# Where x and u tiles begin in the state buffer, against the weights, in a two-layer trunk kernel

## The chip, the cores and the metric

The kernel runs on one core of a Trainium2 chip. The metric is the device time of one execution in microseconds; the time before is the median of three runs, and the profile is one further execution of the same program.

## The reference, cut to what matters

The input is x of 512 frames by 1024 features, float32. Layer 0 is a gated linear recurrence (HGRN2), layer 1 differential attention over one shared K/V; each is followed by a squared-ReLU MLP of width 4096. Every sub-layer has an RMSNorm before and after it.

```
def squared_relu_mlp(h, w_up, w_down):
    u = jax.nn.relu(h @ w_up)
    return (u * u) @ w_down

for layer in range(2):
    mix = hgrn2_mixer(rms_norm(h, a_norm_pre), ...) if layer == 0 else diff_attn_mixer(rms_norm(h, b_norm_pre), k_sh, v_sh, ...)
    h = h + rms_norm(mix, post)
    h = h + rms_norm(squared_relu_mlp(rms_norm(h, mlp_norm_pre[layer]), w_up, w_down), mlp_norm_post[layer])
    if layer == 0:
        k_sh, v_sh = shared_kv(h, kv_norm, w_kv)
```

## The kernel before, in words

Activations are kept transposed: features on the 128 partitions, frames along the row. Every large product is taken in three float32r matmuls, because each operand is split into a rounded part (hi) and the rest (lo): weights hi by x hi, weights hi by x lo, weights lo by x hi (`mm3`). Each of the three loads its 128 by 128 stationary operand anew (LDWEIGHTS) and streams 512 or 256 columns of the moving one.

The tiles that TensorE reads:
- `xhi0..3` and `xlo0..3`, the sub-layer's input, each 128 by 2 by 512 float32, that is 4096 bytes on each partition.
- `uhi0..3` and `ulo0..3`, of the same size: the mixer's output or the MLP's u. `xraw0..3` (the raw input) and `sums1`, `sums2` lie in the same places at the start, and the attention keeps q and k of some heads there.
- `whi` and `wlo`, the split weights, 4096 bytes each, eight buffers of each, in the pool `wp`.
- `t{layer}_{n}`, the block sums of x for three quarters of each MLP's first product, which is taken with seven instead of eight block products (`sums_x`, `Pair`). They lie in the pool of the MLP under the tag `big`. For the first layer's gates and values the block sums lie in buffers of the weights, and one in `uhi3` and `ulo3`.

Tiles are placed one after the other in the order in which they are made, each rounded up to 32 bytes. The pool `cp` holds `gn`, then x, u and small tables, then comes `wp`. In the kernel before, the sizes in `cp` add up so that every tile of x, u, `t` and the weights begins at the same place modulo 512 bytes. A matmul's operands begin at multiples of 512 bytes within their tiles, so the moving operand and the weights that are loaded during it begin at the same place modulo 512 bytes too.

In nearly all these products the weights are stationary and x, u or `t` moves. In the products for the values (`xmm`: tiles `i`, `is`, `v`) x is stationary and the weights move.

The order of the matmuls on TensorE is fixed when the program is written out, by a planner (`Plan`) with estimated durations; the other engines' instructions are put in order by the framework. `by_halves` and the first MLP quarter run over 256 frames at a time; the MLP's second product (`dn`) runs over 512 columns in three quarters of four.

The recurrence of head h ends with three matmuls into the PSUM tile `st{h}`, an ACT copy and two VectorE operations that make the running state `st{h}` in the state buffer (lines 888 to 896, two buffers), and then seven matmuls `o`, three of which read `st{h}` (lines 898 to 903). Heads come in pairs; where both heads of a pair are ready at once, the second head's `st` is made before the first head's `o`.

`ones1` is a 128 by 128 table of ones beside `onesd`, a table of 1/1024. `ones1` serves three small products: line 769 (the first reciprocal norm, spread over the partitions), line 414 (its columns) and line 788 (lambda). Each is copied out of PSUM by VectorE.

Of the kernel before, what the change touches and what calls it, by code (L numbers as in the profile page):

```python
# [9 lines left out]
F32 = mybir.dt.float32  # L10
F32R = mybir.dt.float32r
# [3 lines left out]
ALU = mybir.AluOpType  # L15
AX = mybir.AxisListType

P = 128
D = 1024
S = 512  # L20
# [24 lines left out]
class Plan:  # L45
# [11 lines left out]
    def until(self, *keys):  # L57
        return lambda: all(k in self.done for k in keys)
# [30 lines left out]
def trunk_kernel(ctx: ExitStack, tc: tile.TileContext, x_t, w_qf, w_g, w_gs, w_i, w_is, w_ao, w_kv, w_q, w_bo, w_up, w_us, w_dn,  # L89
# [3 lines left out]
    cp = ctx.enter_context(tc.tile_pool(name="cp", bufs=1))  # L93
# [4 lines left out]
    def mmt(name):  # L98
        return pm.tile([P, 512], F32, tag="mm", name=name, bufs=4)

    def smt(name):
        return pm.tile([P, 512], F32, tag="sm", name=name, bufs=4)

    v, a, g = nc.vector, nc.scalar, nc.gpsimd
# [16 lines left out]


    gn = cp.tile([P, G_N + 14], F32, name="gn")[:, :G_N]
    xhi = [cp.tile([P, 2, S], F32R, name=f"xhi{i}") for i in range(4)]
    xlo = [cp.tile([P, 2, S], F32R, name=f"xlo{i}") for i in range(4)]
    xraw = [cp.tile([P, 2, S], F32, tag=f"uhi{i}", name=f"xraw{i}", bufs=1) for i in range(4)]
    uhi = [cp.tile([P, 2, S], F32R, tag=f"uhi{i}", name=f"uhi{i}", bufs=1) for i in range(4)]
    sums = [cp.tile([P, 4, 256], F32, tag=f"ulo{i}", name=f"sums{i}", bufs=1) for i in (1, 2)]
    ulo = [cp.tile([P, 2, S], F32R, tag=f"ulo{i}", name=f"ulo{i}", bufs=1) for i in range(4)]

    res = [x_t.rearrange("(k p) t -> p k t", p=P)[:, :, lo:hi] for lo, hi in ((0, 256), (256, 512))]
    a.dma_start(gn, gains)
# [1 line left out]
    mask = cp.tile([P, len(LEVELS), 64], U8, name="mask")  # L134
    onesd = cp.tile([P, P], F32, name="onesd")
    v.memset(onesd, 1.0 / D)
    ones1 = cp.tile([P, P], F32, name="ones1")
    v.memset(ones1, 1.0)
    lb = cp.tile([P, NH], F32, name="lb")
    oml = cp.tile([P, NH], F32, name="oml")  # L140
    rb = cp.tile([P, S], F32, name="rb")
    rcol = cp.tile([P, 4], F32, name="rcol")
# [8 lines left out]
    nlam = cp.tile([P, 1], F32, name="nlam")  # L151
# [111 lines left out]
    def mean_cols(parts, n, ones):  # L263

        ps = smt("ps_mc")[:, :n // P]
        for t in range(n // P):
            for i, sq in enumerate(parts):
                pe.matmul(ps[:, t:t + 1], sq[:, t * P:(t + 1) * P], ones[:, 0:1], start=(i == 0), stop=(i == len(parts) - 1))
        return ps
# [15 lines left out]
    def rsqrt_rows(tmp, ms, add):  # L285

        n = ms.shape[1]
        y, t = tmp
        if add is None:
            a.activation(y, ms, AF.Ln, bias=epsc)  # L290
        elif isinstance(add, float):
            x = ms
            a.activation(y, x, AF.Ln)
        else:
            x = add
            v.tensor_tensor(x, ms, add, op=ALU.add)
            a.activation(y, x, AF.Ln)
        a.activation(y, y, AF.Exp, scale=-0.5)
        if add is None:
            v.scalar_tensor_tensor(t, ms, EPS, y, op0=ALU.add, op1=ALU.mult)  # L300
        else:
            v.tensor_tensor(t, x, y, op=ALU.mult)
        v.tensor_tensor(t, t, y, op=ALU.mult)
        v.scalar_tensor_tensor(y, t, -3.0, y, op0=ALU.add, op1=ALU.mult)
        return y

    def bounds(pool, ps_list, zacc, h, gpost, eab, want, name, gpre=None):

        lo, hi = halves[h]
        n = hi - lo  # L310
# [94 lines left out]
        if want == "ea":  # L405

            a.activation(ea[:, lo:hi], ms, AF.Square, scale=math.sqrt(EPS), bias=eps15)
        else:
            s = rsqrt_rows((tmp[:, 3, 0], tmp[:, 3, 1]), ms, None)
            a.activation(rb[:, lo:hi], s, AF.Copy, scale=-0.5)  # L410
            yield W_RSTD
            pc = smt("ps_rc")
            for i in range(n // P):
                pe.matmul(pc[:, i:i + 1], rb[0:1, lo + i * P:lo + (i + 1) * P], ones1[0:1, 0:1], start=True, stop=True)
            v.tensor_copy(rcol[:, lo // P:hi // P], pc[:, :n // P])
        done(("r", name, h))

    def by_halves(wt, xh, xl, name, before_last=()):
# [36 lines left out]
    def block(pool, proj, gpost, name, layer, want):  # L455

        gpre = gn[:, G_MPRE[layer]:G_MPRE[layer] + 8]
        zacc = pool.tile([P, 8, S], F32, name=f"zacc{layer}")
        last_u = []
        h = 0  # L460
        for r in proj:
            if isinstance(r, list):
                spawn(bounds(pool, r, zacc, h, gpost, None, "ea", name, gpre), 0.3)
                h += 1
            else:
                yield r
# [119 lines left out]
        for q in range(4):  # L586
            if q == 0:
                wt = [load_w(w_up[layer, i], 512, None, f"up{layer}_{i}") for i in range(2)]
                for h, (lo, hi) in enumerate(halves):
                    yield until(("x", name, h))  # L590
                    for pr in range(4):
                        ps = mmt(f"up{layer}_{h}_{pr}").rearrange("p (j t) -> p j t", j=2)
                        for j in range(2):
                            n = 2 * pr + j
# [7 lines left out]
            if q < 3:  # L602
                for i in range(2):
# [6 lines left out]
                    for kt, n4 in order:  # L610
                        wmm(pss[n4], wt, kt, n4 * P, uhi, ulo, 0, S, kt == 0, kt == 7)
                        if kt == 7:
                            n = 4 * i + n4
# [6 lines left out]
            else:  # L620
                wt = load_both(w_dn[layer, q], None, f"dn{layer}_{q}_", last_u[0])
                h = 0
# [70 lines left out]
    def squares(hp, xs):  # L693

        sq = [hp.tile([P, 2, S], F32, tag="vt", name=f"sqx{pr}", bufs=3) for pr in range(4)]
        with tc.issue_after(last_split[0].ins):
            for pr in range(4):
                a.activation(sq[pr], xraw[pr], AF.Square)
        for pr in range(1, 4):
            v.tensor_tensor(sq[0], sq[0], sq[pr], op=ALU.add)  # L700
        return sq[0]
# [43 lines left out]
    def start(hp, xs, maskf):  # L745


        lbe = cp.tile([P, NH], F32, name="lbe")
        lbz = cp.tile([P, NH], F32, name="lbz")
        alb = gn[:, G_LB:G_LB + NH]  # L750
        v.tensor_tensor(lbe, alb, alb, op=ALU.subtract)
        a.activation(lbe, lbe, AF.Exp)
        v.reciprocal(lbz, lbe)
        v.tensor_tensor(lbe, lbe, lbz, op=ALU.mult)
        v.tensor_tensor(lb, lbe, lbe, op=ALU.subtract)
        v.tensor_scalar(oml, lb, -1.0, 1.0, op0=ALU.mult, op1=ALU.add)
        v.tensor_copy(mask, maskf)
        yield until("w1")
        ssum = squares(hp, xs)
        yield W_XSUM  # L760
        rsqrt_col(mean_cols([ssum[:, j, :] for j in range(2)], S, onesd), EPS, rcol, aside=True)
        v.tensor_scalar(nrcol, rcol, -1.0, None, op0=ALU.mult)
        done("rcol")

        dg = hp.tile([P, 4, P], F32, tag="os", name="dg", bufs=2)
        v.tensor_tensor(dg, ident.unsqueeze(1).to_broadcast([P, 4, P]), rcol.unsqueeze(2).to_broadcast([P, 4, P]), op=ALU.mult)
        yield W_XRSTD
        ps = smt("ps_sp")
        pe.matmul(ps, ones1, dg.rearrange("p c t -> p (c t)"), start=True, stop=True)
        v.tensor_copy(rb, ps)  # L770
        done("rb")

    def params(hp):

        lp = hp.tile([1, 256], F32, name="lp")
        a.dma_start(lp, lam_p)
        lpv = lp.rearrange("p (a b d) -> p a b d", a=2, b=2)
        pr_ = lpv[:, :, 0, :]
        v.tensor_tensor(pr_, pr_, lpv[:, :, 1, :], op=ALU.mult)
        l2 = hp.tile([1, 2], F32, name="l2")  # L780
        v.tensor_reduce(l2, pr_, axis=AX.X, op=ALU.add)
        a.activation(l2, l2, AF.Exp)
        l1 = hp.tile([1, 1], F32, name="l1")
        v.tensor_tensor(l1, l2[:, 0:1], l2[:, 1:2], op=ALU.subtract)
        v.tensor_scalar(l1, l1, LAM_INIT, -1.0, op0=ALU.add, op1=ALU.mult)
        yield 15.0
        psl = smt("psl")
        pe.matmul(psl[:, 0:1], ones1[0:1, :], l1, start=True, stop=True)
        v.tensor_copy(nlam, psl[:, 0:1])
        v.tensor_scalar(subg, gn[:, G_SUB:G_SUB + 1], 1.0 - LAM_INIT, None, op0=ALU.mult)  # L790
        relt = hp.tile([32, 16], F32, name="relt")
        a.dma_start(relt, rel)
        tb = hp.tile([P, NB], F32, name="tb")
        oht, bw = tb[0:32], tb[64:80]
        a.dma_start(oht, onehot)
        for c0, c1 in ((0, 512), (512, NB)):
            psb = smt(f"psb{c0}")
            pe.matmul(psb[:16, :c1 - c0], relt, oht[:, c0:c1], start=True, stop=True)
            v.tensor_copy(bw[:, c0:c1], psb[:16, :c1 - c0])
        nc.gpsimd.dma_start(bias_dr, bw.unsqueeze(1).to_broadcast([16, NREP, NB]))  # L800
        done("par")

    def hgrn(hp, w0, xs):
# [8 lines left out]
        def head(h, pss):  # L812
# [39 lines left out]
            for li, s in enumerate(LEVELS + (64,)):  # L852
# [4 lines left out]
                ps = None if s == 1 else smt(f"gl_{h}_{s}")  # L857
                if 1 < s <= 64:
                    for c in range(4):
                        pe.matmul(ps[:m, c * 64:(c + 1) * 64], kk[:, c * P:c * P + m], qv[:, c * b:(c + 1) * b, 1, :],  # L860
                                  start=True, stop=True)
# [26 lines left out]
            ps = smt(f"st{h}")  # L888
            for c in range(3):
                pe.matmul(ps[:, c * P:(c + 1) * P], sc[:, 512 + c * P:512 + (c + 1) * P], vt[:, c, hc:hc + P],  # L890
                          start=True, stop=True)
            st = hp.tile([P, 3, P], F32, tag="st", name=f"st{h}", bufs=2)
            a.activation(st[:, 0, :], ps[:, 0:P], AF.Copy)
            for c in range(1, 3):
                v.scalar_tensor_tensor(st[:, c, :], st[:, c - 1, :], tcur[:, c:c + 1], ps[:, c * P:(c + 1) * P],
                                       op0=ALU.mult, op1=ALU.add)
# [142 lines left out]
        for p in range(4):  # L1039
# [18 lines left out]
            if p == 0:  # L1058
# [4 lines left out]
                for tt in range(4):  # L1063

                    ps = (smt if tt < 2 else mmt)(f"i{tt}")
# [9 lines left out]
                for j in range(2):  # L1075
                    ps = mmt(f"g0_{j}")
# [292 lines left out]
```

## Time and profile before

| | |
|---|---|
| median of three runs | 1265.29 us (1264.32 to 1265.73) |
| the profiled execution | 1264.54 us |
| its span, first to last instruction | 1262.7 us |
| PE (matmul) busy | 1242.9 us, 98%, 8440 instructions |
| PEld (weight load) busy | 1138.3 us, 90%, 8440 instructions |
| DVE, ACT, POOL busy | 827.8, 670.5, 96.0 us |
| HBM | 145 MB read, 10 MB written, 123 GB/s over the span |

Of the profiled execution 1.84 us lie outside its span. A matmul's duration in the trace is modelled and longer than its turn, since matmuls are pipelined; what a matmul costs is the step from its start to the next one's.

### The profile page before, as it was taken

What the parts mean: (1) busy time and instruction counts of PE and PEld (TensorE: products, weight loads), DVE (VectorE), ACT (ScalarE), POOL (GpSimd) and SP (SyncE); (2) the same over time, 40 slices, a digit from 0 to 9 for tenths busy, and PEclk for the clock granted to TensorE, in tenths of its full rate; (3) what the DMA queues carried; (4) which work ended last, traced back from release to release, by engine and by line L of the source; (5) the groups of instructions that cost most, each with busy time, mean ns of one, the idle gap of its engine ahead of it and who ended that gap; (6) DMA issues with size and microseconds to landing.
All of it is one profiled execution on the core that took longest, in us unless ns stands there. A gap on an engine that the chain in (4) does not pass through costs nothing.

```text
span 1262.7 us, 21436 instructions
## 1 busy us (share of the span) xinstructions
PE 1242.9 (98%) x8440; PEld 1138.3 (90%) x8440; DVE 827.8 (66%) x1649; ACT 670.5 (53%) x1244; POOL 96.0 (8%) x174
## 2 busy tenths in 40 slices
PE   8999999999999999999999999999999999999996
PEld 7889899999988989989999788889998998988996
DVE  6888887858854735646388977663875463654645
ACT  6455545447742715617356876663783471651732
POOL 0212211110000000000100000001000000000000
PEclk9999999999999999999999999999999999999999
DMA  7225444244266564635525322232425354473621
GB/s 258 86 51 126 101 109 129 81 152 145 99 158 131 173 140 102 198 69 157 178 86 182 117 84 84 84 100 68 163 105 149 100 178 108 118 186 84 172 77 67
DMA packets 56726, 156.44 MB, mean 124 GB/s; under 512 B 6289, under 2 KB 8594, under 8 KB 56626
## 3 DMA queue, kind: packets, MB, share of 16 engines
q1 hardware_dynamic: 45920, 120.34, 30.5%
q0 software_dynamic: 10464, 34.61, 12.8%
q8 instruction: 66, 1.08, 0.3%
q14 instruction: 34, 0.28, 0.1%
q10 hardware_dynamic: 242, 0.13, 0.0%
HBM read 145.35 MB, written 9.70 MB: 123 GB/s over the span
## 4 chain that ended last, share of the span: by engine, by line
PE 88%; DVE 4%; ACT 3%; DMA 2%; issue 2%; POOL 0%; SPq 0%; DVEq 0%; ACTq 0%
PE dn L114 21%; PE ux L114 10%; PE up L114 7%; PE qf L114 6%; PE dn_h L114 6%; PE kq L114 6%; PE uz L114 5%; PE bo_h L114 3%; PE ao_h L114 3%; PE gl L114 3%; PE v L114 2%; PE uy L114 2%; PE g L114 2%; PE i L114 2%; PE lg L114 2%
## 5 line engine op out<-in xcount | busy, mean ns | idle before, releaser
L114 PE MATMUL dn<-uhi,whi_dn 128*128 128x512 f32 x384 | 149.7, 390 | 0.0
L114 PE MATMUL dn<-ulo,whi_dn 128*128 128x512 f32 x384 | 149.5, 389 | 0.0
L114 PE MATMUL dn<-uhi,wlo_dn 128*128 128x512 f32 x384 | 149.4, 389 | 0.0
L201 ACT ACTIVATE whi_a<-raw_a 128x1024 fp32r<-128x1024 f32 x24 | 25.5, 1061 | 116.7 <-PE dn L114 112.7
L114 PEld LDWEIGHTS dn<-uhi,whi_dn 128*128 128x128 f32 x384 | 72.1, 188 | 15.4 <-ACT r L571 0.7
L114 PEld LDWEIGHTS dn<-uhi,wlo_dn 128*128 128x128 f32 x384 | 72.1, 188 | 15.1
L114 PEld LDWEIGHTS dn<-ulo,whi_dn 128*128 128x128 f32 x384 | 72.1, 188 | 14.7
L174 DVE TENSOR_TENSOR wlo_dn<-raw_dn,whi_dn 128x1024 fp32r<-128x1024 f32 x64 | 76.6, 1220 | 6.6 <-ACT whi_dn L173 5.5
L476 DVE TENSOR_TENSOR ulo<-r,uhi 128x1024 fp32r<-128x1024 f32 (+1 forms) x40 | 40.2, 1010 | 59.7 <-ACT uhi L475 59.7
L114 PE MATMUL up<-xhi,whi_up 128*128 128x256 f32 x256 | 73.2, 286 | 0.0
L114 PE MATMUL up<-xhi,wlo_up 128*128 128x256 f32 x256 | 72.4, 283 | 0.0
L114 PE MATMUL up<-xlo,whi_up 128*128 128x256 f32 x256 | 72.4, 283 | 0.0
L173 ACT ACTIVATE whi_dn<-raw_dn 128x1024 fp32r<-128x1024 f32 x64 | 65.7, 1051 | 7.7 <-PE up L114 3.1
L114 PE MATMUL dn_h<-uhi,whi_dn 128*128 128x256 f32 x240 | 68.3, 285 | 0.0
L114 PE MATMUL dn_h<-uhi,wlo_dn 128*128 128x256 f32 x240 | 67.9, 283 | 0.0
L114 PE MATMUL dn_h<-ulo,whi_dn 128*128 128x256 f32 x240 | 67.9, 283 | 0.0
L618 DVE TENSOR_TENSOR zacc<-dn,zacc 128x512 f32<-128x512 f32 x32 | 22.0, 691 | 56.6 <-PE dn L114 56.6
L520 POOL DMA_DIRECT2D raw_s<-in_w_us_dram x24 | 20.8, 865 | 487.0 <-DMA raw_s<-in_w_us_dram 294.4
L114 PE MATMUL qf<-xhi,whi_qf 128*128 128x512 f32 x128 | 52.1, 407 | 1.9 <-ACT whi_qf L667 1.0
L201 ACT ACTIVATE whi_t<-raw_a 128x1024 fp32r<-128x1024 f32 x24 | 25.4, 1060 | 48.7 <-PE dn L114 26.3
L114 PE MATMUL qf<-xlo,whi_qf 128*128 128x512 f32 x128 | 50.1, 391 | 0.3 <-DVE xlo L688 0.3
L114 PE MATMUL qf<-xhi,wlo_qf 128*128 128x512 f32 x128 | 50.2, 392 | 0.0
(533 smaller groups left out, 4153.0 us busy)
## 6 DMA issues: line engine op xcount, KB each, us to landing
raw_dn<-in_w_dn_dram SPq DMA_DIRECT2D x64, 512.0 KB, 4.4
raw_a<-in_w_us_dram SPq DMA_DIRECT2D x24, 512.0 KB, 4.2
raw_s<-in_w_us_dram SPq DMA_DIRECT2D x48, 256.0 KB, 4.3
raw_s<-in_w_us_dram POOLq DMA_DIRECT2D x24, 512.0 KB, 6.4
raw_up<-in_w_up_dram SPq DMA_DIRECT2D x16, 512.0 KB, 4.2
raw_wkv<-in_w_kv_dram SPq DMA_DIRECT2D x16, 512.0 KB, 3.7
raw_qf<-in_w_qf_dram SPq DMA_DIRECT2D x14, 512.0 KB, 4.7
raw_d<-in_w_us_dram SPq DMA_DIRECT2D x12, 512.0 KB, 3.9
```

The source lines that it names most:

```text
L114: nc.tensor.matmul(out, lhsT, rhs, **kw)
L173: last_split[:] = [a.activation(hi, raw, AF.Copy)]
L174: v.tensor_tensor(lo, raw, hi.bitcast(F32), op=ALU.subtract)
L201: a.activation(hi, raw, AF.Copy)
L476: v.tensor_tensor(ulo[pr][:, :, lo:hi], r, uhi[pr][:, :, lo:hi].bitcast(F32), op=ALU.subtract)
L520: g.dma_start(rs, ws[p, :, 0:2, :], accum_op=ALU.add)
L618: v.tensor_tensor(z, pss[n4], z, op=ALU.add)
```

## The change

Tiles of x and u begin at eight places modulo 512 bytes, counted from where the weights begin; filler tiles (`room`) push them there. `xhi{i}` and `xlo{i}` lie at 32, 96, 352 and 416 bytes for i = 0 to 3, `uhi{i}` and `ulo{i}` (with `xraw{i}`) at 64, 160, 256 and 448; the order of the `ulo` tiles becomes 0, 1, 2, 3. In each MLP's pool a filler of 480 bytes behind `zacc` moves everything after it, the block sums `t` among it, to 480 bytes. Room for this comes from `ones1` (512 bytes) and from one of the two `st` buffers (1536 bytes). Where `ones1` was used, `onesd` is, and the copy out of PSUM becomes a multiplication by 1024.

```
-    xhi = [cp.tile([P, 2, S], F32R, name=f"xhi{i}") for i in range(4)]
-    xlo = [cp.tile([P, 2, S], F32R, name=f"xlo{i}") for i in range(4)]
-    xraw = [cp.tile([P, 2, S], F32, tag=f"uhi{i}", name=f"xraw{i}", bufs=1) for i in range(4)]
-    uhi = [cp.tile([P, 2, S], F32R, tag=f"uhi{i}", name=f"uhi{i}", bufs=1) for i in range(4)]
-    sums = [cp.tile([P, 4, 256], F32, tag=f"ulo{i}", name=f"sums{i}", bufs=1) for i in (1, 2)]
-    ulo = [cp.tile([P, 2, S], F32R, tag=f"ulo{i}", name=f"ulo{i}", bufs=1) for i in range(4)]
+    place = [0]
+    def at(byte):
+        n = (byte - place[0]) % 512
+        if n:
+            cp.tile([P, n // 4], F32, name=f"room{len(rooms)}")
+            rooms.append(n)
+        place[0] = byte
+    rooms, xhi, xlo, xraw, uhi = [], [], [], [], []
+    for t, nm in ((xhi, "xhi"), (xlo, "xlo")):
+        for i in range(4):
+            at((32, 96, 352, 416)[i])
+            t.append(cp.tile([P, 2, S], F32R, name=f"{nm}{i}"))
+    for i in range(4):
+        at((64, 160, 256, 448)[i])
+        xraw.append(...)
+        uhi.append(...)
+    sums, ulo = [], []
+    for i in range(4):
+        at((64, 160, 256, 448)[i])
+        if i in (1, 2):
+            sums.append(...)
+        ulo.append(...)
+    at(0)
...
-    ones1 = cp.tile([P, P], F32, name="ones1")
-    v.memset(ones1, 1.0)
...
-                pe.matmul(pc[:, i:i + 1], rb[0:1, ...], ones1[0:1, 0:1], start=True, stop=True)
-            v.tensor_copy(rcol[:, lo // P:hi // P], pc[:, :n // P])
+                pe.matmul(pc[:, i:i + 1], rb[0:1, ...], onesd[0:1, 0:1], start=True, stop=True)
+            v.tensor_scalar(rcol[:, lo // P:hi // P], pc[:, :n // P], float(D), None, op0=ALU.mult)
...
         zacc = pool.tile([P, 8, S], F32, name=f"zacc{layer}")
+        pool.tile([P, 120], F32, name=f"room{layer}")
...
-        pe.matmul(ps, ones1, dg.rearrange("p c t -> p (c t)"), start=True, stop=True)
-        v.tensor_copy(rb, ps)
+        pe.matmul(ps, onesd, dg.rearrange("p c t -> p (c t)"), start=True, stop=True)
+        v.tensor_scalar(rb, ps, float(D), None, op0=ALU.mult)
...
-        pe.matmul(psl[:, 0:1], ones1[0:1, :], l1, start=True, stop=True)
-        v.tensor_copy(nlam, psl[:, 0:1])
+        pe.matmul(psl[:, 0:1], onesd[0:1, :], l1, start=True, stop=True)
+        v.tensor_scalar(nlam, psl[:, 0:1], float(D), None, op0=ALU.mult)
...
-            st = hp.tile([P, 3, P], F32, tag="st", name=f"st{h}", bufs=2)
+            st = hp.tile([P, 3, P], F32, tag="st", name=f"st{h}", bufs=1)
```

## Rows read from the trace of the kernel before

**Rows 1.** The page: busy time of each engine, then slices of PE and its clock.
```profile
PE 1242.9 (98%) x8440; PEld 1138.3 (90%) x8440; DVE 827.8 (66%) x1649; ACT 670.5 (53%) x1244; POOL 96.0 (8%) x174
...
PE   8999999999999999999999999999999999999996
...
PEclk9999999999999999999999999999999999999999
```

**Rows 2.** The chain of waits in pieces: start us, length us, engine, tile, line, instructions.
```profile
734.07 6.83 PE v L114 x57
...
1035.30 43.60 PE dn L114 x192
...
1086.09 2.88 PE ux L114 x24
...
1232.35 15.11 PE dn_h L114 x126
```

**Rows 3.** PE's timeline near 1243 us: start us, duration us, what, shapes.
```profile
1243.46 0.28 PE L114 MATMUL dn_h<-ulo,whi_dn 128*128 128x256 f32 x1
1243.58 0.28 PE L114 MATMUL dn_h<-uhi,wlo_dn 128*128 128x256 f32 x1
1243.70 0.28 PE L114 MATMUL dn_h<-uhi,whi_dn 128*128 128x256 f32 x1
```

**Rows 4.** The weight loads' timeline in the same stretch.
```profile
1243.46 0.19 PEld L114 LDWEIGHTS dn_h<-uhi,wlo_dn 128*128 128x128 f32 x1
1243.58 0.19 PEld L114 LDWEIGHTS dn_h<-uhi,whi_dn 128*128 128x128 f32 x1
```

**Rows 5.** Stretches of a table by windows: us, busy us (instructions) of PE, PEld, DVE, ACT, POOL, then clock and DMA.
```profile
1036.50:1078.90 42.40, 42.40 (x189) 34.99 (x188) 16.51 (x19) 9.06 (x10) 2.59 (x3) 1.00 0.48 113
...
1172.00:1195.00 23.00, 23.00 (x194) 23.00 (x194) 16.47 (x22) 17.14 (x28) 0.86 (x1) 1.00 0.56 155
```

**Rows 6.** PE's timeline at the first matmuls of 512 columns after those of 256.
```profile
1035.13 0.40 PE L114 MATMUL dn<-uhi,whi_dn 128*128 128x512 f32 x1
1035.37 0.40 PE L114 MATMUL dn<-ulo,whi_dn 128*128 128x512 f32 x1
...
1036.52 0.39 PE L114 MATMUL dn<-uhi,whi_dn 128*128 128x512 f32 x1
```

**Rows 7.** PE's timeline behind a pause that ends near 603.7 us.
```profile
604.00 0.29 PE L114 MATMUL ux<-t,wlo_s 128*128 128x256 f32 x1
604.13 0.40 PE L114 MATMUL ux<-t,whi_s 128*128 128x256 f32 x2
604.36 0.28 PE L114 MATMUL ux<-t,wlo_s 128*128 128x256 f32 x1
```

**Rows 8.** Groups of PE instructions by line and tile: busy us, mean ns, idle before.
```profile
L114 PE MATMUL dn<-uhi,whi_dn 128*128 128x512 f32 x384 | 149.7, 390 | 0.0
...
L114 PE MATMUL up<-xhi,whi_up 128*128 128x256 f32 x256 | 73.2, 286 | 0.0
```

**Rows 9.** The chain of waits where both heads of a pair end together, in two places.
```profile
84.60 3.12 PE o L114 x28
...
205.62 3.12 PE o L114 x28
```

**Rows 10.** All engines' timeline at the first of these places.
```profile
83.94 0.28 ACT L893 ACTIVATE st<-st 128x128 f32<-128x128 f32 x1 [0.39 <-PE st L114]
...
84.32 0.86 DVE L895 SCALAR_TENSOR_TENSOR st<-st,tt,st 128x128 f32<-128x128 f32 x3 [0.16 <-ACT st L893]
...
85.77 0.39 PE L114 MATMUL o<-st,q 128*128 128x128 f32 x2
86.00 0.61 PE L114 MATMUL o<-vt,sc 128*128 128x128 f32 x4
86.20 0.28 ACT L635 ACTIVATE os_a<-o 128x128 f32<-128x128 f32 x1 [1.98 <-PE o L114]
...
86.44 0.39 PE L114 MATMUL o<-st,q 128*128 128x128 f32 x2
...
87.37 0.17 DVE L248 TENSOR_SCALAR nx<-ss 128x4 f32<-128x4 f32 x1 [2.19 <-ACT os_a L635]
```

**Rows 11.** Single lines of VectorE: operation, instructions, shortest/median/longest ns, first and last start.
```profile
L770 DVE COPY rb<-ps_sp x1: 686/686/686, 36.9 to 36.9; 128x512 f32<-128x512 f32 x1
...
L640 DVE TENSOR_SCALAR os_a<-o,yh x16: 344/351/352, 89.6 to 272.8; 128x128 f32<-128x128 f32 x16
...
L808 DVE TENSOR_TENSOR g<-g,rb x2: 683/688/692, 74.1 to 80.3; 128x512 f32<-128x512 f32 x2
...
L1081 DVE TENSOR_TENSOR g<-g,eg x2: 684/684/684, 77.0 to 82.1; 128x512 f32<-128x512 f32 x2
```

**Rows 12.** The chain of waits at the start of the kernel.
```profile
2.62 7.05 DMA xraw<-in_x_t_dram
```

More of the change, by code (lines that the diff above doesn't have):

```diff
@@ L123, in trunk_kernel @@
     gn = cp.tile([P, G_N + 14], F32, name="gn")[:, :G_N]
-    xhi = [cp.tile([P, 2, S], F32R, name=f"xhi{i}") for i in range(4)]
-    xlo = [cp.tile([P, 2, S], F32R, name=f"xlo{i}") for i in range(4)]
-    xraw = [cp.tile([P, 2, S], F32, tag=f"uhi{i}", name=f"xraw{i}", bufs=1) for i in range(4)]
-    uhi = [cp.tile([P, 2, S], F32R, tag=f"uhi{i}", name=f"uhi{i}", bufs=1) for i in range(4)]
-    sums = [cp.tile([P, 4, 256], F32, tag=f"ulo{i}", name=f"sums{i}", bufs=1) for i in (1, 2)]
-    ulo = [cp.tile([P, 2, S], F32R, tag=f"ulo{i}", name=f"ulo{i}", bufs=1) for i in range(4)]
+    place = [0]
[12 more added lines that the diff above has]
+        at((64, 160, 256, 448)[i])
+        xraw.append(cp.tile([P, 2, S], F32, tag=f"uhi{i}", name=f"xraw{i}", bufs=1))
+        uhi.append(cp.tile([P, 2, S], F32R, tag=f"uhi{i}", name=f"uhi{i}", bufs=1))
+    sums, ulo = [], []
+    for i in range(4):
+        at((64, 160, 256, 448)[i])
+        if i in (1, 2):
+            sums.append(cp.tile([P, 4, 256], F32, tag=f"ulo{i}", name=f"sums{i}", bufs=1))
+        ulo.append(cp.tile([P, 2, S], F32R, tag=f"ulo{i}", name=f"ulo{i}", bufs=1))
+    at(0)
     res = [x_t.rearrange("(k p) t -> p k t", p=P)[:, :, lo:hi] for lo, hi in ((0, 256), (256, 512))]
@@ L413, in bounds @@
             for i in range(n // P):
-                pe.matmul(pc[:, i:i + 1], rb[0:1, lo + i * P:lo + (i + 1) * P], ones1[0:1, 0:1], start=True, stop=True)
-            v.tensor_copy(rcol[:, lo // P:hi // P], pc[:, :n // P])
+                pe.matmul(pc[:, i:i + 1], rb[0:1, lo + i * P:lo + (i + 1) * P], onesd[0:1, 0:1], start=True, stop=True)
+            v.tensor_scalar(rcol[:, lo // P:hi // P], pc[:, :n // P], float(D), None, op0=ALU.mult)
         done(("r", name, h))
```

## The prediction

> **What bounds the kernel now.** I read the page first: PE is busy for 98% of the span and at 9 tenths in nearly every slice, with the granted clock at 1.00, the 2.4 GHz level [rows 1]. So there are no gaps worth filling, and the only thing that can move this kernel far is the step from one matmul to the next. The reader should therefore not look at a matmul's 0.28 or 0.39 us, which overlap, but divide stretches of the chain of waits by their instructions [rows 2]: `dn` takes 43.60 / 192 = 227.1 ns for 512 columns; `ux` 2.88 / 24 = 120.0 and `dn_h` 15.11 / 126 = 119.9 ns for 256 columns; `v`, where x is stationary and the weights move, 6.83 / 57 = 119.8 ns. The difference of 107.1 ns for 256 columns is 0.418 ns a column, one column per cycle of the granted clock. What is left is 120.0 - 256 x 0.418 = 12.9 ns that each matmul costs beside its columns, the same for both widths. The change can only work on these 12.9 ns. The starts of matmuls and weight loads show what happens in them: a matmul and the load for the next one start together every 0.12 us [rows 3, 4], so both operands are read at the same time, and in the kernel before both reads begin at the same place modulo 512 bytes.
>
> **The tiles' places: how many matmuls.** Counted from the loops and checked on the counts of two groups [rows 8]. With 512 columns: `dn` 3 x 384 = 1152, `qf` 384, the attention's `kq` 288, `i` 96, `g` 48, together 1968. With 256 columns: `up` 3 x 256 = 768, the six quarters with seven products 24 x 7 x 12 = 2016, `dn_h` with `dn_last` 768, `ao` and `bo` 768, `v` 384, `kq` by halves 192, and 216 of the 420 for the first layer's gates and values; the other 204 move block sums that lie among the weights and keep distance 0. Together 5112. At the steps above these 7080 matmuls are 1968 x 0.2271 + 5112 x 0.1200 = 447 + 613 = 1060 us of the span of 1262.7. One nanosecond on each of them is 7.1 us. About 0.2%, or 2.5 us, is what a measurement of this kernel can tell from no change; it is reached at 0.35 ns a matmul.
>
> **What a new distance costs.** The trace of before holds next to nothing at other distances, so I bound it from both sides.
> From the side of no effect: at distance 0 the step doesn't care how hard the state buffer is read by others. From 1172 to 1195 us DVE is busy 16.5 and ACT 17.1 of 23 us, from 1036.5 to 1078.9 us 16.5 and 9.1 of 42.4 [rows 5], and the steps in both kinds of stretch are the settled 120 and 227 ns. If reads collided by address, these engines, which run through the same places, would blur PE's step. It also doesn't matter which operand is x: 119.8 against 120.0 ns.
> From the dear side: the step isn't a constant of the matmul. The first six of 512 columns after those of 256 take (1036.52 - 1035.13) / 6 = 231.7 ns [rows 6], 4.6 more than settled ones, with no wait between them. And after a pause a matmul of 256 columns took 130 ns [rows 7]. If every one came at the dear step: 1968 x 4.6 + 5112 x 10 = 9 + 51 = +60 us.
> From the cheap side: the two after that one took (604.36 - 604.13) / 2 = 115 ns [rows 7]. If every matmul lost 5 ns: 7080 x 5 = -35 us. The 12.9 ns as a whole would be -91 us, but no row shows a float32r matmul near that.
> Dear and cheap ones follow each other in the same few matmuls (130, 115, 115: mean 120), and the nearest rows to the value that I need are the settled ones, whose only flaw is that they all have one distance. I take 0 for the tiles' places, and keep both ends for the range.
>
> By the Trainium skill, TensorE has two SBUF read ports of its own, one for the moving operand and one for the weight load, and loading the next weights takes no read bandwidth from the running matmul ("TensorE: Matmul & The Clock Gate", Step-by-step: what each phase is for). By that rule the distance changes nothing, which is my 0; the trace agrees in that other engines leave the step alone, and doesn't show the ports.
> The same page (Back-to-back issue gap) gives a warm gap of N / 2.4 + 2.5 ns, 215.8 and 109.2 ns here; the trace shows 227.1 and 120.0. By it 11.3 x 1968 + 10.8 x 5112 = 77 us are lost to something that the page doesn't name, and a distance that cured it would give 1187 us. I hold this against my 0, not as a forecast.
>
> **One `st` buffer less.** In two places both heads of a pair end together [rows 9]. There the second head's copy (ACT, 83.94) and its VectorE operations (in the group at 84.32) are done before the first head's `o` [rows 10]. With one buffer they must wait until the first head's last read of `st` is through, that is after the pair of matmuls at 85.77, whose 0.39 us end at 86.16. Then come ACT 0.28 and VectorE 0.34 twice (0.86 us is three overlapped). TensorE wants the first piece at 86.44: it would be there about 86.5, the later ones 0.1 to 0.2 late. Queued behind the waiting copy on ACT is `os_a`, before which ACT idles 1.98 us, and behind the VectorE operations `nx`, with 2.19 us idle: that idle time hides the wait, and what is late next is the first head's norm by 0.3 us. I take 0.25 us twice, +0.5; the bounds are 0 and the whole chain twice, 2 x (0.28 + 2 x 0.34) = 1.9 us. The other pairs make their states one at a time.
>
> **Ones, copies, other engines.** One memset goes, off the path. The copies become multiplications out of PSUM: 686 ns for the copy of 512 columns, 351 for a multiplication of 128 [rows 11]; the difference is 0.87 ns a column over 384 columns, what reading columns costs, so 0 (at worst some 0.1 us, four times). VectorE reads at other distances already: `rb` begins at 448 bytes modulo 512, and a product with it takes 688 ns against 684 with a tile at its side [rows 11]. The first load of x lands at another place in its row; it is on the chain for 7.05 us [rows 12], and I take 0, between -0.3 and +0.5 us.
>
> **Sum.** Against the profiled execution (1262.7 span and 1.84 around it, 1264.54): 0 + 0.5 + 0 = 1265.0 us. The median of the runs lies 0.75 us above that execution, so the forecast is 1265.8 us.
>
> **Rivals.**
> *The settled step is lost (slower).* Place: each change of tile, which comes every six matmuls (two feature blocks by three), or 24 in the first half of `dn`. Each matmul of 512 columns then costs what unsettled ones cost, +9.1 us, and of those with 256 one in six the dear 130 ns: 5112 / 6 x 10 ns = +8.5 us. With 0.5 this is 1284 us. For it: a settled step exists, takes about six matmuls to come back, and came about with one distance throughout. Against it: at 256 columns the unsettled ones average the settled 120 ns. It decides from 0.35 ns a matmul on.
> *Beginning at the same place is what costs the 12.9 ns (faster).* Both reads start together at the same place, and a tile at another distance would escape. If half of the distances give the cheap 115 ns and the same 5 ns at 512 columns, 3540 x 5 = -17.7 us: 1248 us. For it: 12.9 ns at both widths, which is a fixed loss per load. Against it: the loss stays the same whatever the neighbours do, and the new places could be as bad.
> *The change does nothing where it says.* This is inside the forecast: the `st` wait alone decides, 1265 to 1268 us.
>
> **How the numbers follow.** Forecast (no effect, or dear and cheap steps that cancel) 0.38, of which 0.29 within 0.2%, 0.07 slower and 0.02 faster; its own range is 1264 to 1269 us. Lost step 0.35, all slower. Escaped collision 0.27, of which 0.26 faster and 0.01 within 0.2%. So faster 0.28, within 0.2% 0.30, slower 0.42. The range takes the forecast whole and the two rivals to about one and a half times their prices: 1240 to 1292 us, which leaves out the full dear and cheap ends.
>
> **What would show it.** In the profile after, divide `dn` by its instructions: 227 ns in every stretch means that the distance is nothing; a step that differs between stretches with `uhi0` to `uhi3`, or between x tiles, means that it is something, and the list of steps by tile tells which distance is good. The unsettled starts should look as before. The chain should show a wait of `o` for `st` near 86.5 and 207.5 us, 0.1 to 0.5 us each. I am wrong if PE's busy time moves by more than 3 us with no new wait.

## The result, and the profile after

The changed kernel takes 1268.58 us (median of 20 runs, 1266.22 to 1270.01), the kernel before, run beside it, 1265.23 us (20 runs, 1264.23 to 1267.28). The ratio is 1.0026 with a 95% interval of 1.0019 to 1.0033: slower by 3.3 us, only just more than the 2.5 us that can be told from no change. The profiled execution of the changed kernel took 1266.22 us (span 1264.4); it is the quickest of the 20, so its span is only 1.7 us above that of the kernel before, not 3.3.

The page, with the same lines as [rows 1]: busy time of each engine, and slices of PE and its clock.

```profile
PE 1244.4 (98%) x8440; PEld 1131.3 (89%) x8440; DVE 828.8 (66%) x1648; ACT 670.5 (53%) x1244; POOL 95.5 (8%) x174
...
PE   9999999999999999999999999999999999999996
...
PEclk9999999999999999999999999999999999999998
```

Nothing seems to have happened: PE has the same 8440 instructions, one VectorE instruction (the memset) is gone, the clock is at 2.4 GHz as before. The chain of waits, which answers to [rows 2], shows that something has (start us, length us, engine, tile, line, instructions):

```profile
407.66 2.85 PE ux L114 x24
...
735.85 6.79 PE v L114 x57
...
1037.04 44.44 PE dn L114 x192
...
1234.29 14.79 PE dn_h L114 x126
```

Divide as before. `dn`, 512 columns, takes 44.44 / 192 = 231.5 ns where it took 227.1; `dn_h`, 256 columns, 14.79 / 126 = 117.4 where it took 119.9; `ux` 118.8 (120.0), `v` 119.1 (119.8). Wide matmuls became dearer and narrow ones cheaper. The groups say the same with less contrast, because a matmul's own duration overlaps the next one (against 390 and 286 ns in [rows 8]; last columns: busy us, mean ns, idle before):

```profile
L114 PE MATMUL dn<-uhi,whi_dn 128*128 128x512 f32 x384 | 150.9, 393 | 0.0
...
L114 PE MATMUL up<-xhi,whi_up 128*128 128x256 f32 x256 | 72.5, 283 | 0.0
```

Adding up all steps of the two traces from one matmul's start to the next (the order of the matmuls on PE is the same, so they can be subtracted one by one; steps above 170 ns at 256 columns and 250 ns at 512 count as waits) gives the account of TensorE: 1884 steps of 512 columns +7.76 us, 5212 of 256 columns -8.21, the two waits of `o` for `st` +0.89, other waits +0.82, the rest +0.31; together +1.57 us. So the places cost -0.45 us on balance, out of two terms of nearly 8 us each. Divided by operand, the products with u come to +1.4 us and those with x and the block sums to -1.9.

The two waits for `st` answer to [rows 9]: the chain there was one piece of 28 `o`, and is now broken after 14. The chain of waits at the first place, and all engines' timeline around it ([rows 10]):

```profile
85.20 1.57 PE o L114 x14
...
86.97 0.20 ACT os_a L654
87.17 0.17 ACT st L912
...
87.39 1.38 PE o L114 x10
```

```profile
86.60 0.61 PE L114 MATMUL o<-vt,sc 128*128 128x128 f32 x4
86.80 0.28 ACT L654 ACTIVATE os_a<-o 128x128 f32<-128x128 f32 x1 [2.66 <-PE o L114]
86.97 0.20 ACT L654 ACTIVATION_READ_ACCUMULATOR os_a<-o 128x1 f32 x1
87.06 0.27 ACT L912 ACTIVATE st<-st 128x128 f32<-128x128 f32 x1
...
87.39 0.49 PE L114 MATMUL o<-st,q 128*128 128x128 f32 x2 [0.18 <-ACT st L912]
87.42 0.73 DVE L914 SCALAR_TENSOR_TENSOR st<-st,tt,st 128x128 f32<-128x128 f32 x2 [2.47 <-ACT st L912]
```

In the kernel before, the copy to `st` (ACT, 0.28 us) ran ahead of both heads' `o`. With one buffer it not only waits for the first head's last read: it also stands behind that head's first `os_a`, whose activation and read of the accumulator take until 87.17; the copy begins at 87.06. The first `o` that needs the second `st` starts at 87.39; by its step in the two traces (454 ns here, 112 before) that is 0.34 us later than without the wait, and the next one loses another 0.10: 0.44 us at each of the two places.

Of the other edits: the multiplication that replaced the copy of 512 columns takes 684 ns against 686 [rows 11], and the products `g` take 684 to 692 ns with `rb` and 684 to 686 with a tile beside it, as before; `rb` itself begins at 448 bytes in both kernels. The first load of x took 6.73 us on the chain against 7.05 [rows 12]. The multiplication, from VectorE's single lines (operation, shortest/median/longest ns, first and last start):

```profile
L789 DVE TENSOR_SCALAR rb<-ps_sp x1: 684/684/684, 36.9 to 36.9; 128x512 f32<-128x512 f32 x1
```

### The profile page after: what moved, and what is told of

Read it like the earlier page. It is cut to its first block, busy times and chain, and to the rows that moved or that the text cites. A ratio compares the mean times of both kernels' runs of the same rounds, so it can differ in the third digit from the quotient of the medians.

```text
span 1264.4 us, 21437 instructions
## 1 busy us (share of the span) xinstructions
PE 1244.4 (98%) x8440; PEld 1131.3 (89%) x8440; DVE 828.8 (66%) x1648; ACT 670.5 (53%) x1244; POOL 95.5 (8%) x174
## 4 chain that ended last, share of the span: by engine, by line
PE 88%; issue 4%; ACT 3%; DMA 2%; DVE 2%; POOL 1%; SPq 0%; DVEq 0%; ACTq 0%; POOLq 0%
PE dn L114 21%; PE ux L114 10%; PE up L114 7%; PE qf L114 7%; PE kq L114 6%; PE uz L114 5%; PE bo_h L114 3%; PE ao_h L114 3%; PE dn_h L114 3%; PE gl L114 3%; PE v L114 3%; PE uy L114 2%; PE g L114 2%; PE lg L114 2%; PE i L114 2%
```

## The experiments

Two questions: is it the distance between the operands that changes the step, and why did a change of 7000 steps come out at nearly nothing? Where steps are given by distance below, they are worked out from the starts of the matmuls in the trace: the mean from the tenth matmul on, in stretches of one distance and one width without waits. A kernel's filler behind `zacc` is set so that the block sums lie where x lies (480 bytes where x has four distances); that line of its edit is left out below.

**All distances undone** (`e1_no_distances`): the changed kernel with every tile back at the weights' place.

```diff
-        at((32, 96, 352, 416)[i])
+        at((0, 0, 0, 0)[i])
...
-        at((64, 160, 256, 448)[i])
+        at((0, 0, 0, 0)[i])
```

> The changed kernel with every tile back at distance 0: what is left are the one st buffer and the missing table of ones. Theory (two effects of the distances nearly cancel, the dear steps at 512 columns and the cheap ones at 256, and the st waits come on top): about 0.9 us above the kernel before, for the two waits of o for st, with dn back at 227.1 ns and dn_h at 119.9 ns a matmul. Rival (the distances do nothing, the small edits are the whole loss): 3.3 us above, like the changed kernel.

Measured: 1267.7 us against 1265.82 (ratio 1.0009, 0.9999 to 1.0019). The chain of waits is back at the steps of before: 15.11 us for 126 `dn_h`, 43.60 for 192 `dn`.

```profile
1121.23 43.60 PE dn L114 x192
...
1233.96 15.11 PE dn_h L114 x126
```

So the steps follow the distances. In the times, some 0.0017 of the 0.0026 goes with them, and what is left is about 1 us by the ratio; the medians lie 1.9 us apart, and the interval allows 0 to 2.4.

**One distance for all of x** (`e2_x_448`), **and for x and u** (`e3_all_448`): x and the block sums at 448, in the second kernel u too, and two `st` buffers again in both.

```diff
-        at((32, 96, 352, 416)[i])
+        at((448, 448, 448, 448)[i])
...
-        at((64, 160, 256, 448)[i])
+        at((0, 0, 0, 0)[i])          # e3_all_448: (448, 448, 448, 448)
...
-            st = hp.tile([P, 3, P], F32, tag="st", name=f"st{h}", bufs=1)
+            st = hp.tile([P, 3, P], F32, tag="st", name=f"st{h}", bufs=2)
```

> x and the block sums all at 448 bytes, u at 0, two st buffers. Theory (each distance has a step of its own that matmuls settle at when the distance stays the same; in the changed kernel runs at 448 settle at 113.3 ns for 256 columns and 233.3 ns for 512): 3084 matmuls of 256 columns gain 6.67 ns, 720 of 512 lose 6.67, 456 with x stationary gain 2.2: -20.6 + 4.8 - 1.0 = -16.8 us, 1248.5 us. Rival (what costs is the change of distance from tile to tile; with one distance, whichever, the steps settle at 120 and 227): 1265 us.

> x, u and the block sums all at 448 bytes, two st buffers. Theory (a step of its own for each distance): beside the 16.8 us of x, 1536 matmuls with u of 256 columns gain 6.67 ns (-10.2) and 1152 of 512 columns lose 6.67 (+7.7): 1246 us, with dn at 233.3 and dn_h at 113.3 ns. Rival (only the change from tile to tile matters): 1265 us, dn at 227.

Measured: 1260.49 us (ratio 0.9957, 0.9944 to 0.9970) and 1260.13 (0.9959, 0.9943 to 0.9974). Both are faster than the kernel before, so a single distance does not simply settle at the old step; but the gain is 5 us and not 17 to 20. The chain of waits of `e3_all_448` shows one reason. These are the same instructions with the same tiles' places in the kernel's two feed-forward layers:

```profile
310.74 16.34 PE up L114 x144
...
327.67 23.13 PE up L114 x204
...
906.09 16.96 PE up L114 x144
...
923.48 24.03 PE up L114 x204
...
1032.27 44.80 PE dn L114 x192
...
1203.56 26.52 PE dn_h L114 x234
...
1230.51 14.84 PE dn_h L114 x126
```

In the first layer `up` runs at 16.34 / 144 = 113.5 and 23.13 / 204 = 113.4 ns, in the second at 117.8 and 117.8; `dn_h` at 113.3 for 234 matmuls and, after a pause, 117.8 for 126. At distance 0 all of these are 120 (17.27 / 144, 24.47 / 204). So at one distance a stretch can settle at either of two steps, and stays there until something interrupts it. And 512 columns are dear at 448: 44.80 / 192 = 233.3 ns, +7.25 us for all `dn`. The other reason is waits: the steps of `e3_all_448` come to -21.1 us at 256 columns (-31.8 forecast) and +9.9 at 512, but 8.4 of the 11.2 us gained are lost again in longer waits, most of it at the place that is shown for `e8_all_64` below. In `e2_x_448` the steps gain 10.0 us and waits take 3.0. The theory of one step for each distance was half right; the rival, that only the change of tile unsettles the step, is out.

**Five more distances** (`e4_scan`): u at 32, 96, 128 and 192, x and the block sums at 320.

```diff
-        at((32, 96, 352, 416)[i])
+        at((320, 320, 320, 320)[i])
...
-        at((64, 160, 256, 448)[i])
+        at((32, 96, 128, 192)[i])
```

> One look: u0 to u3 at 32, 96, 128 and 192 bytes, x and the block sums at 320, one st buffer. Long runs with one u tile (24 matmuls of 512 columns in the first half of dn, 48 of 256 in the first half of dn_h) show the settled step of each distance. Theory (a step of its own for each distance): steps that differ from tile to tile, between 113 and 120 ns and between 220 and 238 ns, each run settling to one value or a short repeating row. Rival (settling at 120 and 227 whatever the distance): every long run ends at 120 and 227.

Measured: 1266.19 us in one run (kernel before 1265.82). Settled steps in ns, with those of the other kernels (352 and 416 have no stretch that is long enough; the block sums at 480 settle at 118.1 ns):

```
distance        0      32     64          96     128    160    192         256    320         448
256 columns     120.0  116.6  113.3|117.8 120.0  118.6  117.6  113.3|117.8 120.0  113.3|117.8 113.3|117.8
512 columns     226.7  233.2  228.9       233.5  233.2  234.2  233.3       226.7  228.9       233.3
```

Two things stand out: 0 and 256 are alike, so are 64 and 320, and so are 192 and 448; and no distance is better than 0 at 512 columns, while none of them is worse at 256 columns.

**Half of the change undone** (`e5_u_undone`: u back at 0; `e6_x_undone`: x back at 0).

```diff
-        at((64, 160, 256, 448)[i])
+        at((0, 0, 0, 0)[i])          # e5_u_undone
...
-        at((32, 96, 352, 416)[i])
+        at((0, 0, 0, 0)[i])          # e6_x_undone
```

> The u tiles go back to distance 0, the x tiles keep the change's four distances. Theory (each distance has its own step and the terms add): dn falls from 231.6 to 227.2 ns (-5.05 us), dn_h rises from 117.9 to 120.5 (+1.9), what moves x stays as in the changed kernel: 1268.6 - 5.05 + 1.9 = 1265.4 us, span near 1261. Rival (the loss of the changed kernel has nothing to do with the distances): 1268 us or more, as the changed kernel itself.

> The other half: x tiles at distance 0, u tiles at the change's four distances. Theory: dn stays at 231.6 ns and dn_h at 117.9; qf, kq, i and g lose the 2.1 us that they gained in length, and up, ux, uy, uz and v give back some 3.6 to 4 us: 1268.6 - 2.1 + 3.8 = 1270.3 us, the slowest of all. Rival (terms do not add, a step depends on what ran before it as much as on its distance): between 1264 and 1268 us, with dn or dn_h off these values by over 2 ns.

Measured, each against the runs of the kernel before beside it (1266.22 us, where these two took 1267.08 and 1268.96), with the two kernels that complete the square:

```
                     x at 0                          x at four distances
u at 0               1.0009 (0.9999 to 1.0019)       1.0008 (0.9999 to 1.0017)
u at four distances  1.0026 (1.0015 to 1.0037)       1.0026 (1.0019 to 1.0033)
```

What is lost in the times goes with the u tiles: 0.0017 to 0.0018, 2.2 us, where each ratio is good to about 0.001. x's distances cost and gain nothing in the times, though their steps gain 1.9 us. The steps, here as means with all pauses, came as the theory said: `dn` 227.2 with u undone and 231.8 without, `dn_h` 120.5 and 117.9. Of u's tiles the steps of the changed kernel add up to dn +5.05, dn_h -1.88, the attention's projections `ao_h` and `bo_h` -1.43 and their last parts -0.2, together +1.5 us. `e5_u_undone` was forecast at 1265.4 us and took 1267.08: its steps came as forecast, but in its profiled execution the waits beside those for `st` are 3.7 us longer than in the kernel before. `e6_x_undone` was forecast as the slowest at 1270.3 us and is not slower than the changed kernel (1.0026 both): a miss of some 1.8 us; the last experiment shows waits that vary by as much between two executions.

**Better places** (`e7_x_320`: like `e2_x_448` with 320 for 448; `e8_all_64`: like `e3_all_448` with 64).

```diff
-        at((448, 448, 448, 448)[i])
+        at((320, 320, 320, 320)[i])  # e7_x_320, from e2_x_448
...
-        at((448, 448, 448, 448)[i])
+        at((64, 64, 64, 64)[i])      # e8_all_64, from e3_all_448, both lines
```

> x tiles and the block sums at 320 instead of 448, u at 0, two st buffers. Theory (at 512 columns the settled step is 228.9 at 320 and 233.3 at 448, at 256 columns the two distances share the steps 113.3 and 117.8): 816 matmuls of 512 columns move x, at most 816 x 4.4 = 3.6 us less than with 448, about 2 us by what qf and kq lost there: 1258.5 us (1256.9 to 1260). Rival (the step at 512 columns is set by the order of the tiles, not by the distance): 1260.5 us as with 448, qf and kq at the same steps.

> x, u and the block sums at 64, two st buffers. Theory: dn settles at 228.9 ns (+2.0 us against the kernel before, where 448 gave +7.25), qf, kq, i and g likewise; 256 columns settle at 117.8 or 113.3 (5112 x 2.2 = 11.2 us less at the first of them throughout, half of that by what 448 gave): 1265.2 + 3.3 - 5.6 to 11.2 = 1257 to 1263 less what the lower step adds, 1255 us as the middle. Rival (only a distance of 448, just ahead of the weights, is cheap; 64 is no better than 0): 1265 us, ux, up and dn_h at 120 ns.

Measured: 1260.84 us (ratio 0.9957, 0.9945 to 0.9970; 1258.5 forecast) and 1259.45 (0.9950, 0.9937 to 0.9962; the kernel before 1266.22). `e8_all_64` is some 6 us faster than the kernel before and 9 us faster than the changed one, and its rival, that only 448 is cheap, is out. Its chain of waits, and a stretch in which a pair of blocks waits for its weights:

```profile
309.75 16.32 PE up L114 x144
...
326.52 24.03 PE up L114 x204
...
1114.99 39.65 PE dn L114 x173
...
1200.58 27.56 PE dn_h L114 x234
```

```profile
492.65 7.39 DMA raw_s<-in_w_us_dram
...
500.12 1.07 ACT whi_s L219
...
501.21 1.23 DVE wlo_s L220
502.44 0.34 DVE r L585
...
502.82 0.39 PE ux L114
```

`dn` settles at 39.65 / 173 = 229.2 ns as forecast, `up` at 113.3 or 117.8, `dn_h` at 27.56 / 234 = 117.8. But the steps' gain isn't the kernel's gain: the steps come to -12.3 us, and waits take back 7.8. Of these, 5.9 us are six pauses of PE behind `uz`. VectorE's addition for `r`, which frees the PSUM tile that `ux` needs, stands behind the split of the next weights (`wlo_s`), which needs ScalarE's `whi_s`, which needs a load on GpSimd's queue that takes 7.4 us. TensorE now comes to that place earlier than the load. The same eats the forecast of `e7_x_320`, whose time alone would fit its rival: `qf` and `kq` at 512 columns lost 0.70 us instead of 2.47 with 448, as the theory said, yet `uz` with its pauses took 2.4 us more than in the kernel before, and more narrow stretches fell to the dearer of the two steps.

Is it the distance between the operands that counts, or just the place of the tile of x or u? In `i` (512 columns) x is stationary and the weights move, which lie at 0 in every kernel, so its distance is the other way round. The chain of waits of `e3_all_448` (x at 448, so the distance is 64) and of `e8_all_64` (x at 64, so it is 448):

```profile
35.93 11.00 PE i L114 x48
```

```profile
35.46 11.20 PE i L114 x48
```

That is 229.2 and 233.3 ns, while `dn`, with stationary weights, has 233.3 in the first kernel and 229.2 in the second. The step goes with the distance.

**The leftover** (`e9_st_alone`: the kernel before with one `st` buffer; `e10_two_st`: the changed kernel with no distances and two).

```diff
-            st = hp.tile([P, 3, P], F32, tag="st", name=f"st{h}", bufs=2)
+            st = hp.tile([P, 3, P], F32, tag="st", name=f"st{h}", bufs=1)   # e9_st_alone
...
-            st = hp.tile([P, 3, P], F32, tag="st", name=f"st{h}", bufs=1)
+            st = hp.tile([P, 3, P], F32, tag="st", name=f"st{h}", bufs=2)   # e10_two_st, from e1_no_distances
```

> The kernel before with one st buffer and nothing else of the change. Theory (what is left over when all distances are undone is the wait for st, two waits of 0.45 us): o +0.9 us, 1266.1 us where the kernel before takes 1265.2, ratio 1.0007. Rival (the leftover comes from the copies that became multiplications or from the missing table of ones): ratio 1.0000, o at 109.3 ns as before with no wait for st on the chain.

> The changed kernel with all distances undone and two st buffers: only the missing table of ones and the multiplications by 1024 are left. Theory (the wait for st is the leftover): ratio 1.0000 to the kernel before, o at 109.3 ns, 1265.2 us. Rival (the multiplications or the table cost it): ratio 1.0009, 1266.3 us, and a longer pause of TensorE around ps_rc, ps_sp or psl.

Measured: ratio 1.0007 (0.9998 to 1.0016) and 1.0003 (0.9994 to 1.0012). Neither can be told from 1 by the times alone, but the values are those of the theory, and the chain decides the place: with one buffer (first fence, the kernel before with that edit) the pieces of 28 `o` break after 14 at both places, with two (second fence) they are whole again. The steps of `o` sum to +0.89 us in `e9_st_alone` and 0.00 in `e10_two_st`.

```profile
84.42 1.57 PE o L114 x14
...
205.92 1.57 PE o L114 x14
```

```profile
84.67 3.12 PE o L114 x28
...
206.77 3.12 PE o L114 x28
```

**The changed kernel once more** (`e11_after_look`), with no edit.

> The changed kernel again, for a second profile beside the one of 1264.4 us span, which is 2.3 us below its median. Theory (the steps belong to the distances and repeat): dn at 231.6 ns and dn_h at 117.9 again within 0.2 ns, and what differs in time lies in waits, at the start or in stretches of lower granted clock. Rival (the steps come out another way in each execution): dn or dn_h off by over 1 ns.

Measured: 1268.65 us, span 1266.8, which is 2.4 us above the first profile and at the median of its runs. The steps repeat: `dn`, `dn_h`, `up` and `ux` differ from the first profile by 0.02, 0.00, -0.12 and 0.17 us in all. The 2.4 us are waits, two of them large: +1.35 us before `gl` near 141 us and +1.17 before `ux` at 1189.7. The chain of waits at both:

```profile
127.94 10.12 DMA raw_tis<-in_w_is_dram
...
1179.29 7.62 DMA raw_s<-in_w_us_dram
...
1186.98 1.07 ACT whi_s L219
...
1188.07 1.23 DVE wlo_s L220
1189.30 0.34 DVE r L585
...
1189.69 2.41 PE ux L114 x18
```

In the first profile the chain ran through PE alone at both places, and the same two loads took 8.8 and 6.5 us where they take 10.1 and 7.6 here. A load that lands later pushes a VectorE queue, and that pushes PE. This is where the two executions differ, by about as much as the change is worth.

## Why the prediction came out

**The time.** Forecast 1265.8 us, measured 1268.58; inside the likeliest case's own range (1264 to 1269). The verdict, slower by 0.26%, falls to the part of that case that had a chance of 0.07; the whole chance given to slower was 0.42. Of the 3.3 us the forecast had 0.5, for `st`.

**The bound.** Right: with PE at 98% the steps decide. It was right to expect no gain from anything else. What it left out is that shorter steps can lengthen waits: `e8_all_64` loses 7.8 of 12.3 us in this way.

**How many matmuls.** 1968 of 512 and 5112 of 256 columns were forecast; by the operands' addresses 1978 and 5146 have a distance other than 0.

**What a new distance costs.** The value, 0, was nearly met (-0.45 us), the alternative reason named beside it in the forecast held (dear and cheap steps cancel), and the one it leaned on did not. That the sum comes near 0 is luck: the prediction priced no width by itself, and other places take 5 to 6 us off the same kernel. By the sign that the prediction set (`dn` at 227 ns in every stretch would mean that the distance is nothing), its reason failed: the settled steps of 120 and 227 ns belong to distance 0. The prediction's sentence that their only flaw is that they all have one distance named the hole. "Dear and cheap ones follow each other" was read off a transient [rows 7]; what cancelled were two widths: +7.76 us at 512 and -8.21 at 256 columns. The dear row of 231.7 ns [rows 6] is near the 231.5 to which `dn` went, but by chance: it was read at distance 0, and 231.5 is a mean over four distances with settled steps from 226.7 to 234.2. The cheap row of 115 ns, also from distance 0, lies in the same way among the steps between 113.3 and 118.6 that most distances give. That neighbouring engines don't disturb the step says nothing about the distance between the two operands of one matmul: that was the wrong inference.

By the Trainium skill ("TensorE: Matmul & The Clock Gate", Step-by-step: what each phase is for) loading the next weights takes nothing from the running matmul, because it has a read port of its own. The prediction took from it that the distance changes nothing. No run here shows the ports, but the runs refute what was taken from the rule: with the same instructions in the same order, the step at 512 columns goes from 227.1 to 233.3 ns and at 256 columns from 120.0 to 113.3 when the operands' places change. The measurement decides. By the same page of the Trainium skill (Back-to-back issue gap) the gap of an isolated matmul is 109.2 ns at 256 columns and 215.8 at 512, an estimate worked out from its formula; the Trainium skill sets it apart there from a stream in which each matmul has a weight load, as here, so the 77 us that the prediction made of it are no loss that it states. The best settled step in any run here is 113.3 ns at 256 columns, and none at 512 is below 226.7.

**The `st` buffer.** Predicted +0.5, measured +0.89. The wait is where it was expected; its size was off, because the prediction let the copy start when `o` was through (86.16 in the times of before) and put `os_a` behind it. (It also read the second head's VectorE operations as done before the first head's `o`; the group at 84.32 in [rows 10] ends at 85.18, and the piece of `o` in [rows 9] begins at 84.60.) The trace has the first `os_a` in front of it: 0.44 us at each place, within the bounds of 0 to 1.9.

**Ones, copies, first load.** Zero each, as forecast, within what can be seen: `e10_two_st` holds just these edits, 1.0003 (0.9994 to 1.0012).

**The rivals.** "The settled step is lost" was right in kind for 512 columns (+9.1 forecast, +7.76 measured) and wrong for 256 (+8.5 forecast, -8.21), where new settled steps are cheaper than the old; and not the change of tile but the distance does it, since `e3_all_448` has one distance and 233.3 ns. "Beginning at the same place is what costs the 12.9 ns" was right in sign for 256 columns and wrong for 512. Each rival described one width and was priced on both. (The sum of the first, +9.1, +8.5 and +0.5 on 1265.3, is 1283.4 and not 1284.)

**What stays open.** Why the step depends on the distance, and what decides which of 113.3 and 117.8 ns a stretch falls into, no run here shows. The 3.3 us are not fully accounted for either. By the steps the change costs 0.4 us: -0.45 for the places and +0.89 for `st`. By the times 2.2 us go with u's distances, of which 1.5 are seen as steps, and the 1.9 us that x's steps gain do not arrive. The rest lies in waits: in the second profile of the changed kernel, which is as slow as the median, those beside the waits for `st` are 3.7 us longer than in the kernel before, in the first 0.8. Which of them come with the places and which with the execution, no run separates.

## What to carry to other kernels

Where TensorE is busy throughout, divide a stretch of the chain by its instructions, for each width apart, before and after any change of where tiles lie: a kernel can gain 8 us and lose 8 us and show nothing on the page. Places are a parameter to try, with one distance for all tiles of an operand so that its steps can be read (here 64 or 448 for what runs at 256 columns, 0 for 512), and not a mix of eight, which averages the good with the bad. That choice by width was not run; the four kernels with one distance for x took 0.4 to 0.5% off, and their intervals overlap. Read the waits along with the steps, since what the steps gain can come back as waits for loads. A value taken from a trace in which the changed quantity never varied is a guess, whatever its precision.

## What the runs showed of the hardware

- The step of float32r matmuls depends on the distance between the start of the moving operand and that of the stationary one, here counted modulo 512 bytes: the settled steps are 113.3 to 120.0 ns at 256 columns and 226.7 to 234.2 at 512, all at a granted clock of 1.00. It is the distance and not the place of one tile: with x stationary and the weights moving, x at 448 and at 64 change roles (229.2 and 233.3 ns for `i`, 233.3 and 229.2 for `dn`).
- Four of the settled values are a whole multiple of 16 cycles of 2.4 GHz above the columns: 272 / 2.4 = 113.3, 288 / 2.4 = 120.0, 544 / 2.4 = 226.7, 560 / 2.4 = 233.3. The other two frequent ones, 117.8 and 228.9, are means of short patterns (such as 117, 118, 118, 117, 119 in `e3_all_448`, and 226, 229, 232, 225, 230, 231 in `e8_all_64`).
- At most distances the step gets dearer at 512 columns and cheaper at 256 (64: 228.9, and 113.3 or 117.8). In the three pairs that are 256 bytes apart (0 and 256, 64 and 320, 192 and 448) both have the same steps.
- One distance can have two settled steps at 256 columns, 113.3 and 117.8 ns; no uninterrupted stretch changed from one to the other, and after a pause it can be either (`dn_h` in `e3_all_448`).
